# Moving the stationary operands of a two-layer decoder trunk to a pool of their own in SBUF

## The chip, the cores and the metric

The kernel runs on one core of one Trainium2 chip. The metric is the device time of one execution in microseconds (us); lower is better. Three runs of the kernel before gave 948.11 us as their median (947.25 to 948.29).

## The reference

Two layers over 256 tokens of width 1024, all in float32. Every matrix product of a layer is, cut to what matters:

```python
h = rms_norm(x, norm_mix_pre)
proj = h @ w_in                       # 1024 x 8208: conv, retention, GLA inputs and three merge gates
y_a, y_b, y_c = short_conv(...), retention(...), gated_linear_attention(...)   # 512 wide each
merged = sum(sigmoid(gate_i) * (y_i @ w_branch_i))
x = x + rms_norm(merged @ w_out, norm_mix_post)
h = rms_norm(x, norm_ffn_pre)
x = x + rms_norm((silu(h @ w_gate) * (h @ w_up)) @ w_down, norm_ffn_post)      # 2816 wide
```

## The kernel before

The 256 tokens are two row tiles of 128, t = 0 and t = 1. A product keeps the activations stationary and streams the weights: `mm` (line 272) calls one matmul with a stationary block of 128 x 128 and a moving block of 128 x 512 weights (256 or 272 at the edge of a matrix).

Precision comes from splitting. Activations and weights each become a high part (`hi`, float32r) and the rest (`lo`), and each block of 128 rows takes three matmuls: hi x whi, hi x wlo, lo x whi (`piece`, line 379). So each of these matmuls has its own stationary load, and successive matmuls use the blocks hi[i], hi[i], lo[i], hi[i+1], ...

The stationary tiles are:

- `hT0hi`, `hT0lo`, `hT1hi`, `hT1lo`: the transposed activations of row tile 0 and 1, eight blocks of 128 x 128 each (4096 bytes in a partition), one buffer each. They hold the normalised h, and later the merged m.
- `yThi`, `yTlo`: transposed branch outputs and the SwiGLU activations, four blocks each (2048 bytes), four buffers each. The GLA factors (`factors`, line 740) borrow the same buffers.

`pair` (line 413) makes both kinds; `sb` (line 241) makes the scratch tiles and the GLA factors under the tags `yThi` and `yTlo`:

```python
def sb(tag, bufs, cols=512, dt=F32):
    return p1.tile([P, cols], dt, tag=tag, name=nm(tag), bufs=bufs)
def pair(kt, tag, bufs):
    return [p1.tile([P, kt, P], F32R, tag=tag + s, name=nm(tag + s), bufs=bufs) for s in ("hi", "lo")]
```

Weights arrive in units of 512 KB (128 x 1024 float32) on SP's DMA queue into four `raw` buffers. ScalarE copies a unit to `whi` (line 189), VectorE writes the rest to `wlo` (line 191), in eight buffers each. A unit of 1024 columns feeds 12 matmuls, six for each row tile.

The order of TensorE's and SP's instructions is written out by the program itself (`Order`, a small planner that puts transposes and the chunk products of the branches between the pieces of the large products). ScalarE, VectorE and GpSimd are ordered by the framework. In most of the program a piece for t = 0 is followed by one for t = 1 on the same weights. In the closing of each half layer (`closing`) and the opening of the next (`skewed`) one row tile runs several pieces ahead of the other, so that stretches use hT0 alone or hT1 alone.

SBUF is laid out pool after pool, each pool's tags in the order of their first use: `const`, `rawp`, `wp`, `p1`, `sm`.

Of the kernel before, what the change touches and what calls it, by code (L numbers as in the profile page):

```python
# [10 lines left out]
F32R = mybir.dt.float32r  # L11
# [6 lines left out]
P = 128  # L18
# [202 lines left out]
def trunk(ctx: ExitStack, tc: tile.TileContext, ins, out):  # L221
# [2 lines left out]
    TS = range(NT)  # L224

    const = ctx.enter_context(tc.tile_pool(name="const", bufs=1))
    raw_pool = ctx.enter_context(tc.tile_pool(name="rawp", bufs=NRAW))
    wpool = ctx.enter_context(tc.tile_pool(name="wp", bufs=NSLOT))
    p1 = ctx.enter_context(tc.tile_pool(name="p1", bufs=1))
# [7 lines left out]
    def nm(s):  # L237
        cnt[0] += 1
        return f"{s}_{cnt[0]}"

    def sb(tag, bufs, cols=512, dt=F32):
        return p1.tile([P, cols], dt, tag=tag, name=nm(tag), bufs=bufs)

    def gt(cols=512):
        return sb("gt", 5, cols)

    def ut(cols=512):
        return sb("ut", 4, cols)

    def long():  # L250
        return sb("long", 6)
# [159 lines left out]
        return a, V.tensor_tensor(flat(lo[:, c0:c0 + n, :]), src, ho.bitcast(F32), ALU.subtract)  # L411

    def pair(kt, tag, bufs):
        return [p1.tile([P, kt, P], F32R, tag=tag + s, name=nm(tag + s), bufs=bufs) for s in ("hi", "lo")]

    def T_task(src, dst, wait, c0=0, n=4):
        yield wait
# [9 lines left out]
    def renorm(t, banks, w_post, w_next=None):  # L427
# [28 lines left out]
        if w_next is None:  # L456
            return
        yield CHAIN - HOLD
        hT[t] = pair(8, f"hT{t}", 1)
        for nb in range(2):  # L460
            yield O.acquire("tp")
# [83 lines left out]
    def first_norm(t, wait):  # L545
        yield wait
        hT[t] = pair(8, f"hT{t}", 1)
        hi, lo = hT[t]
        last = first_split[t]
        for c in range(2):  # L550
            yield O.acquire("ac")
            tp = transposed(x_sb[t][:, c * 512:(c + 1) * 512], 4, "ac")
            with tc.high_priority(offset=FIRST_PRI[t]):
                h = ut()
                V.tensor_tensor(h4(h), h4(tp), w_col[:, 4 * c:4 * c + 4].unsqueeze(2).to_broadcast([P, 4, P]), ALU.mult)
                last.append(split(h, hi, lo, 4 * c))
            O.release("ac", 1, 1.6)
            W.urgent = list(last[-1])
            W.split()
        W.hold = 1 - t  # L560
# [18 lines left out]
    for l in range(DEPTH):  # L579
# [337 lines left out]
        yT = [[None, None] for _ in range(3)]  # L917
# [19 lines left out]
        def conv_gate_task(t, b, conv):  # L937
            yield 1.5
            yield lambda: conv.done
            yield O.acquire("tp")  # L940
            tp = transposed(b)
            V.tensor_tensor(y_a[t], y_a[t], tp, ALU.mult)
            O.release("tp", 1, 2.0)
            yT[0][t] = pair(4, "yT", 4)
            split(y_a[t], *yT[0][t])
# [33 lines left out]
        for br in range(3):  # L979
            sig = {}  # L980
            for nb in range(2):
                for t, acc in enumerate(block()):
                    s = ut()
# [110 lines left out]
```

## Time and profile before

| what | value |
|---|---|
| median of the runs | 948.11 us (947.25 to 948.29) |
| the profiled execution | 948.13 us |
| its span, first to last instruction | 946.4 us |
| TensorE busy | 922.2 us, 97% of the span |
| VectorE, ScalarE, GpSimd busy | 61%, 49%, 11% |
| mean granted TensorE clock | 0.993 |
| moved by DMA | 165.67 MB, 175 GB/s on average |

The profile's times of matmuls overlap: one is shown with 0.39 us, but the next starts 0.23 us after it. How fast TensorE works is read from the distance of the starts in the timeline, or from a piece of the chain of waits, divided by its count.

### The profile page before, as it was taken

Reading aid. Unit: us, or ns where it says so; the run is one execution under the profiler, and the core shown is the slowest. Engines: PE = TensorE matmul, PEld = TensorE weight load, DVE = VectorE, ACT = ScalarE, POOL = GpSimd, SP = SyncE. Lnnn points to the kernel's source line nnn. Section 1 sums busy time; section 2 is a strip of 40 time slices with the busy share of each in tenths; the row PEclk is TensorE's granted clock in tenths of the full one; section 3 lists DMA queues with packets and bytes.
Section 4 is the critical chain, followed back from the end, with each engine's and each line's share of the span. In section 5 each row is a group of like instructions: output and inputs, shape, how many; then the busy total and the mean of one; then the engine's idle time right before and its main releaser. Section 6 shows DMA issues by size and latency. Waiting matters only on the chain.

```text
span 946.4 us, 12659 instructions
## 1 busy us (share of the span) xinstructions
PE 922.2 (97%) x4831; PEld 753.9 (80%) x4831; DVE 580.0 (61%) x830; ACT 462.1 (49%) x612; POOL 100.2 (11%) x142
## 2 busy tenths in 40 slices
PE   7889999999999999999989999999999999999997
PEld 5768888888888888888978778888888888888895
DVE  6789768555477655455466976775456765455443
ACT  5664364544456544444457536454444564444431
POOL 9022121002000000000010333010020000000000
PEclk9899999999999999999999999999999999999999
DMA  9985468868536767655679446788765476566621
GB/s 205 218 206 153 99 181 187 207 184 192 178 93 201 252 187 223 185 185 188 135 110 231 132 133 134 182 241 182 182 194 163 126 233 208 179 202 185 192 90 45
DMA packets 89485, 165.67 MB, mean 175 GB/s; under 512 B 5777, under 2 KB 15057, under 8 KB 89425
## 3 DMA queue, kind: packets, MB, share of 16 engines
q1 hardware_dynamic: 88192, 162.94, 64.6%
q0 software_dynamic: 656, 1.62, 0.7%
q8 instruction: 38, 0.62, 0.3%
q10 hardware_dynamic: 576, 0.30, 0.2%
q14 instruction: 23, 0.18, 0.1%
HBM read 163.79 MB, written 1.05 MB: 174 GB/s over the span
## 4 chain that ended last, share of the span: by engine, by line
PE 87%; DMA 5%; DVE 5%; issue 2%; ACT 1%; POOL 1%; POOLq 0%; DVEq 0%; ACTq 0%
PE mm L273 65%; PE ac L273 19%; DMA raw<-in_w_in_dram 5%; PE tp L279 3%; DVE wlo L191 2%; POOL gt L813 1%; ACT whi L189 1%; DVE yTlo L752 0%; DVE yThi L753 0%; DVE S L736 0%; DVE gt L811 0%; DVE x L447 0%; DVE gt L808 0%; DVE glo L690 0%; POOL rs L377 0%
## 5 line engine op out<-in xcount | busy, mean ns | idle before, releaser
L191 DVE TENSOR_TENSOR wlo<-raw,whi 128x1024 fp32r<-128x1024 f32 (+2 forms) x303 | 370.1, 1227 | 288.6 <-ACT whi L189 288.0
L189 ACT CAST whi<-raw 128x1024 fp32r<-128x1024 f32 (+2 forms) x303 | 314.7, 1040 | 348.1 <-PE mm L273 239.6
L273 PE MATMUL mm<-whi,hT1hi 128*128 128x512 f32 (+2 forms) x464 | 179.8, 388 | 1.8 <-ACT hT1hi L410 1.0
L273 PE MATMUL mm<-whi,hT0hi 128*128 128x512 f32 (+2 forms) x464 | 178.8, 385 | 1.1 <-ACT whi L189 1.1
L273 PE MATMUL mm<-wlo,hT0hi 128*128 128x512 f32 (+2 forms) x464 | 176.4, 381 | 0.5 <-DVE wlo L191 0.3
L273 PE MATMUL mm<-wlo,hT1hi 128*128 128x512 f32 (+2 forms) x464 | 176.8, 382 | 0.0
L273 PE MATMUL mm<-whi,hT1lo 128*128 128x512 f32 (+2 forms) x464 | 176.5, 380 | 0.2 <-DVE hT1lo L411 0.2
L273 PE MATMUL mm<-whi,hT0lo 128*128 128x512 f32 (+2 forms) x464 | 176.6, 381 | 0.0
L273 PEld LDWEIGHTS mm<-whi,hT1hi 128*128 128x128 f32 x464 | 87.8, 189 | 19.9 <-ACT hT1hi L410 1.2
L273 PEld LDWEIGHTS mm<-whi,hT0hi 128*128 128x128 f32 x464 | 88.6, 191 | 18.6 <-ACT whi L189 1.6
L273 PEld LDWEIGHTS mm<-wlo,hT0hi 128*128 128x128 f32 x464 | 88.6, 191 | 18.5 <-DVE wlo L191 1.9
L273 PEld LDWEIGHTS mm<-whi,hT1lo 128*128 128x128 f32 x464 | 87.5, 188 | 18.5 <-DVE hT1lo L411 0.5
L273 PEld LDWEIGHTS mm<-whi,hT0lo 128*128 128x128 f32 x464 | 88.4, 191 | 17.0
L273 PEld LDWEIGHTS mm<-wlo,hT1hi 128*128 128x128 f32 x464 | 87.5, 189 | 16.3
L273 PE MATMUL ac<-whi,yThi 128*128 128x512 f32 x176 | 71.3, 405 | 0.0
L273 PE MATMUL ac<-whi,yTlo 128*128 128x512 f32 x176 | 69.5, 395 | 0.0
L273 PE MATMUL ac<-wlo,yThi 128*128 128x512 f32 x176 | 69.3, 394 | 0.0
L377 POOL TENSOR_TENSOR rs<-rs,mhalf 128x1 f32<-128x1 f32 (+1 forms) x24 | 17.3, 719 | 442.5 <-DVE rs L439 441.2
L273 PEld LDWEIGHTS ac<-whi,yTlo 128*128 128x128 f32 x176 | 33.1, 188 | 7.7
L273 PEld LDWEIGHTS ac<-wlo,yThi 128*128 128x128 f32 x176 | 33.3, 189 | 6.8
L273 PEld LDWEIGHTS ac<-whi,yThi 128*128 128x128 f32 x176 | 33.2, 189 | 6.7
L273 PE MATMUL mm<-whi,yThi 128*128 128x512 f32 x96 | 38.2, 398 | 0.0
(169 smaller groups left out, 898.1 us busy)
## 6 DMA issues: line engine op xcount, KB each, us to landing
raw<-in_w_in_dram SPq DMA_DIRECT2D x123, 512.0 KB, 4.9
raw<-in_w_ffn_gate_dram SPq DMA_DIRECT2D x44, 512.0 KB, 3.7
raw<-in_w_ffn_up_dram SPq DMA_DIRECT2D x44, 512.0 KB, 4.3
raw<-in_w_ffn_down_dram SPq DMA_DIRECT2D x44, 512.0 KB, 3.8
raw<-in_w_out_dram SPq DMA_DIRECT2D x16, 512.0 KB, 4.0
raw<-in_w_branch_a_dram SPq DMA_DIRECT2D x8, 512.0 KB, 8.7
raw<-in_w_branch_b_dram SPq DMA_DIRECT2D x8, 512.0 KB, 4.1
raw<-in_w_branch_c_dram SPq DMA_DIRECT2D x8, 512.0 KB, 3.5
```

The source lines that it names most:

```text
L189: nc.scalar.copy(hi[:, c], raw[:, c])
L191: nc.vector.tensor_tensor(lo[:, c], raw[:, c], hi[:, c].bitcast(F32), ALU.subtract)
L273: T.matmul(acc, lhsT, rhs, start=start, stop=stop)
L279: T.transpose(acc, src, ident)
L377: return G.tensor_tensor(v, v, mhalf[:, :n], ALU.pow)
L813: last = G.tensor_tensor(a, a, b, ALU.add)
```

## The change

A pool `stat` is opened between `const` and `rawp`. All tiles of `pair`, and those of `sb` whose tag begins with `yT`, are taken from it. Tags, sizes and numbers of buffers stay.

```diff
     const = ctx.enter_context(tc.tile_pool(name="const", bufs=1))
+    stat = ctx.enter_context(tc.tile_pool(name="stat", bufs=1))
     raw_pool = ctx.enter_context(tc.tile_pool(name="rawp", bufs=NRAW))
...
     def sb(tag, bufs, cols=512, dt=F32):
-        return p1.tile([P, cols], dt, tag=tag, name=nm(tag), bufs=bufs)
+        return (stat if tag[:2] == "yT" else p1).tile([P, cols], dt, tag=tag, name=nm(tag), bufs=bufs)
...
     def pair(kt, tag, bufs):
-        return [p1.tile([P, kt, P], F32R, tag=tag + s, name=nm(tag + s), bufs=bufs) for s in ("hi", "lo")]
+        return [stat.tile([P, kt, P], F32R, tag=tag + s, name=nm(tag + s), bufs=bufs) for s in ("hi", "lo")]
```

No instruction moves: on all five engines the built programs have the same instructions in the same order with the same waits (PE, DVE, ACT, POOL and SP alike). Only addresses differ. The first byte of each tile in its partition, in the two built programs, and how far that lies past a multiple of 512 bytes (the size of one stationary block):

| tile | before | past 512 | after | past 512 |
|---|---|---|---|---|
| hT0hi, hT0lo | 132608, 136704 | 0 | 38400, 42496 | 0 |
| hT1hi, hT1lo | 141888, 145984 | 64 | 46592, 50688 | 0 |
| yThi (four, 2048 apart) | 197248 | 128 | 54784 | 0 |
| yTlo (four, 2048 apart) | 205440 | 128 | 62976 | 0 |
| raw (four, 4096 apart) | 38400 | 0 | 71168 | 0 |
| whi (eight, 4096 apart) | 54784 | 0 | 87552 | 0 |
| wlo (eight, 4096 apart) | 87552 | 0 | 120320 | 0 |
| ut (four, 2048 apart) | 120320 | 0 | 153088 | 0 |
| xs | 150080, 154208 | 64, 96 | 166464, 170592 | 64, 96 |
| qkT, gt, long, ghi, glo | from 158336 | 128 | from 174720 | 128 |
| S, nw, const, sm | | | not moved | |

So hT1, yThi and yTlo are the only tiles whose distance past a multiple of 512 changes; each 512-byte block of a tile has its tile's distance.

## Rows read from the trace of the kernel before

**Rows 1.** The page: span, busy time and share, granted clock in tenths
```profile
span 946.4 us, 12659 instructions
...
PE 922.2 (97%) x4831; PEld 753.9 (80%) x4831; DVE 580.0 (61%) x830; ACT 462.1 (49%) x612; POOL 100.2 (11%) x142
...
PEclk9899999999999999999999999999999999999999
```
**Rows 2.** What TensorE waited for: us in total, times, longest us
```profile
PE tp L279 <- ACT ut L595: 4.9, 1, 4.9
PE ac L273 <- ACT gaT L676: 2.6, 1, 2.6
...
PE mm L273 <- DVE hT1lo L411: 0.2, 1, 0.2
```
**Rows 3.** The chain that ended last, by time: start us, us, what
```profile
8.42 7.97 DMA raw<-in_w_in_dram
...
46.67 9.37 DMA raw<-in_w_in_dram
...
201.00 58.52 PE mm L273 x252
...
476.80 10.45 DMA raw<-in_w_in_dram
```
**Rows 4.** TensorE's groups by shape: count | busy us, mean ns | idle before
```profile
L273 PE MATMUL mm<-whi,hT1hi 128*128 128x512 f32 x400 | 161.6, 404 | 1.8 <-ACT hT1hi L410 1.0 <-ACT long L595 0.8
L273 PE MATMUL mm<-whi,hT0hi 128*128 128x512 f32 x400 | 159.1, 398 | 1.1 <-ACT whi L189 1.1
...
L273 PE MATMUL ac<-whi,yThi 128*128 128x512 f32 x176 | 71.3, 405 | 0.0
...
L273 PE MATMUL mm<-whi,yThi 128*128 128x512 f32 x96 | 38.2, 398 | 0.0
...
L273 PE MATMUL mm<-whi,hT0hi 128*128 128x256 f32 x48 | 15.1, 314 | 0.0
...
L273 PE MATMUL ac<-whi,hT1hi 128*128 128x512 f32 x32 | 13.0, 406 | 0.0
```
**Rows 5.** Timeline of TensorE, first layer's `w_out` product: start us, us, instruction
```profile
269.02 0.60 PE L279 MATMUL tp<-ident,xs 128*128 128x128 f32 x4
269.37 0.48 PE L273 MATMUL ac<-whi,hT0hi 128*128 128x512 f32 x1
269.69 0.40 PE L273 MATMUL ac<-wlo,hT0hi 128*128 128x512 f32 x1
...
272.23 0.39 PE L273 MATMUL ac<-whi,hT0hi 128*128 128x512 f32 x1
...
276.31 0.40 PE L273 MATMUL ac<-whi,hT1hi 128*128 128x512 f32 x1
276.54 0.39 PE L273 MATMUL ac<-wlo,hT1hi 128*128 128x512 f32 x1
...
280.97 0.39 PE L273 MATMUL ac<-whi,hT1lo 128*128 128x512 f32 x1
```
**Rows 6.** Timeline of TensorE, first branch product: start us, us, instruction
```profile
184.66 0.39 PE L273 MATMUL mm<-whi,yThi 128*128 128x512 f32 x1
...
195.82 0.39 PE L273 MATMUL mm<-whi,hT0hi 128*128 128x512 f32 x1
```
**Rows 7.** Timeline of TensorE, a w_in product, row tiles in turn
```profile
127.75 0.39 PE L273 MATMUL mm<-whi,hT1hi 128*128 128x512 f32 x1
...
129.15 0.39 PE L273 MATMUL mm<-whi,hT0hi 128*128 128x512 f32 x1
...
130.53 0.39 PE L273 MATMUL mm<-whi,hT1hi 128*128 128x512 f32 x1
```
**Rows 8.** Busy us of each engine from 201.0 to 259.5, clock, DMA share, GB/s
```profile
201.00:259.50 58.50, 58.50 (x255) 47.31 (x254) 29.34 (x29) 25.58 (x28) 6.91 (x4) 1.00 0.69 185
```
**Rows 9.** Timeline of all engines at 130 us: a matmul and stationary loads
```profile
130.30 0.39 PE L273 MATMUL mm<-whi,hT0lo 128*128 128x512 f32 x1
130.31 0.19 PEld L273 LDWEIGHTS mm<-whi,hT1hi 128*128 128x128 f32 x1
...
130.54 0.19 PEld L273 LDWEIGHTS mm<-wlo,hT1hi 128*128 128x128 f32 x1
```
**Rows 10.** Timeline of TensorE, last gate product, 256 columns wide
```profile
451.04 0.28 PE L273 MATMUL mm<-whi,hT1hi 128*128 128x256 f32 x1
...
452.46 0.28 PE L273 MATMUL mm<-whi,hT0hi 128*128 128x256 f32 x1
...
453.90 0.28 PE L273 MATMUL mm<-whi,hT1hi 128*128 128x256 f32 x1
```

## The prediction, made before the changed kernel ran

> **What bounds the kernel now.** I read the page first: TensorE is busy 922 of 946 us at nearly full granted clock [rows 1]. The table of TensorE's waits comes next: twelve entries of one wait each, from 4.9 us down to 0.2, 17.7 us together [rows 2]. The chain of waits then shows where the end is set: apart from weight DMAs in the first 56 us and at the change of layers, it consists of long pieces of matmuls, such as 252 of them in 58.52 us [rows 3]. So the time is the number of matmuls times the distance between their starts, and only something that alters that distance matters.
>
> That distance is what to look at. [...] The piece holds products on hT0, hT1 and yT, and no engine is short there: VectorE 29.3 us, ScalarE 25.6 us of 58.5, DMA 0.69 [rows 8].
>
> The timeline then tells the three stationary operands apart. In one product (same function, same kind of weights, same width) hT0 alone goes from 272.23 to 276.31, 18 matmuls in 4.08 us: 226.7 ns each. Directly behind it hT1 alone goes from 276.54 to 280.97, 19 distances in 4.43 us: 233.2 ns [rows 5]. yT alone takes 48 matmuls from 184.66 to 195.82: 232.5 ns [rows 6]. At 256 columns the two row tiles differ as well, but the other way round: 12 on hT1 take 1.42 us (118.3 ns), 12 on hT0 1.44 us (120.0 ns) [rows 10]. The next stationary load starts with the running matmul, 10 ns after it, and so reads SBUF while the weights stream out of it [rows 9]. What differs between the three operands is where they lie: hT0 at a multiple of 512 bytes, hT1 64 bytes past one, yT 128 past one. All weight tiles lie at multiples of 512.
>
> I read this as two reads of SBUF that get in each other's way by their relative position. [...] It isn't the accumulator: all eight blocks of a tile, weights in any of the 16 weight buffers, and other accumulators show the same 226 to 227 ns once hT0 has run alone for some ten matmuls.
>
> **The change part by part.** No instruction is added, removed or moved, and no wait differs. No DMA moves past another on any queue. Only three operands change their position against the weights: hT1 and yT come to lie as hT0 does, at a multiple of 512. hT0, the weights and the sources of the transposes (ut, xs, gt, long) keep theirs.
>
> *The term that pays.* Matmuls with 512 columns: hT0 and hT1 have three groups each of 400 and of 32, that is 2592; yT three groups each of 176 and of 96, 816; together 3408 [rows 4]. They come in 107 uninterrupted stretches (my count in the timeline); the first of each waits for its own load, as the 320 ns from 269.37 to 269.69 show [rows 5], and the last is cut off by what follows, so about 3200 distances count. If all are locked as hT0 alone is, each loses 232.2 - 226.7 = 5.5 ns: 3200 x 5.5 = 17.6 us.
>
> *What is taken off.* The 226.7 isn't there at once. Behind four transposes, the eleven distances from 269.69 to 272.23 take 2.54 us, 46 ns more than at 226.7 [rows 5]. Each of the 107 stretches starts so: 107 x 0.046 = 4.9 us. In the first 56 us and at the layer change, the weight DMA ends last [rows 3]; some 150 matmuls there only wait longer for it: 150 x 5.5 ns = 0.8 us. The 256-wide matmuls on hT1, 3 x 48 as on hT0 [rows 4], become as slow as hT0's: 144 x 1.7 ns = 0.2 us. Left: 17.6 - 4.9 - 0.8 - 0.2 = 11.7 us.
>
> *What hides nothing.* A faster TensorE asks for weights 2% sooner. In the long piece the DMA share goes from 0.69 to about 0.71, and VectorE and ScalarE stay at half [rows 8], so I price a new wait for weights at nothing. If that cover failed, all of the gain would be lost, not more. The 17.7 us of TensorE's waits stay.
>
> *Bounds.* No row shows a stationary tile low in SBUF next to weights that lie just above it, and part of `wlo` now lies beyond 131072 bytes. From below I bound the distance by the 226.7 ns of hT0 for every matmul, without any start of a stretch: 17.6 us gained. From above, by the worst lock that the rows show, 233.2 ns for all: 3200 x (233.2 - 232.2) = 3.2 us lost. I take the value next to hT0, since the position against the weights becomes exactly hT0's.
>
> The profiled execution took 948.13 us, 1.7 beyond its span and as long as the median of 948.11. So 946.4 - 11.7 + 1.7 = 936.4 us.
>
> [...]
>
> **The rivals.**
>
> [...]
>
> *No lock when tiles alternate.* In the w_in product where hT0 and hT1 take turns, six matmuls on hT1 take 1.40 us (233.3 each) and six on hT0 1.38 (230 to 231.3) [rows 7]: hT0 doesn't reach 226.7 there. I put that down to the phase that hT1 leaves behind. If instead any change of tile restarts it, every product would run at about 231.3: 3200 x 0.9 = 2.9 us gained, 945.2.
>
> [...]
>
> *Only h gains* (yT is locked by something of its own, since its buffers change every four blocks): 2592 / 3408 of the gain, 8.9 us: 939.2.
>
> **How the numbers follow.** My forecast has 0.68 (931 to 941 us), only h gains 0.07, no lock 0.07, no say 0.08, slower 0.10. This measurement tells some 0.2%, 1.9 us, from no change. Faster by more than that: 0.68 + 0.07 and most of "no lock", 0.81. Within it: 0.09. Slower: 0.10. The range leaves out the no-change and slower cases, 0.18 together: from 929, a little below 17.6 us gained, to 947.
>
> **What would show it.** Right: the stretch of 252 matmuls takes about 57.2 us; hT1 alone and yT alone show 226 to 227 ns a start after some ten matmuls; the mean times of the groups on hT1hi and yThi (404 and 405 ns [rows 4]) fall towards the 0.39 us of the locked hT0 rows [rows 5]; the waits stay near 17.7 us; the 256-wide matmuls show 120 ns on both tiles. Wrong: distances on hT1 or yT at 232 to 234 as before (position isn't it), or at 226.7 with new waits on `whi` or `wlo` that eat the gain (the cover failed), or hT0's own distances above 227 (the new neighbourhood).

## The result, and the profile after

The changed kernel took 939.74 us (median of three, 938.26 to 940.09) against 948.11: a ratio of 0.990, 95% interval 0.9876 to 0.9923. The forecast was 936.4 us. Two things are to be explained: that the distance between matmuls did what was forecast, almost to the nanosecond, and that 3.3 us of the gain are missing all the same. One execution among all that follow (the third of e10_rel32) took 1300.14 us at a mean granted clock of 0.654, and the comparisons leave it out.

The page of the profile after, the same lines as [rows 1]:

```profile
span 938.4 us, 12659 instructions
...
PE 913.2 (97%) x4831; PEld 756.3 (81%) x4831; DVE 578.9 (62%) x830; ACT 462.8 (49%) x612; POOL 99.4 (11%) x142
...
PEclk9879999999999999999999999999999999999999
```

TensorE is busy 9 us less for the same 4831 instructions, and one of the 40 slices, the third, has a lower clock than before (7 against 9). The timeline of TensorE in the product of [rows 5], each row a start in us, how long the matmul is shown, and the instruction:

```profile
273.84 0.39 PE L274 MATMUL ac<-wlo,hT0hi 128*128 128x512 f32 x1
...
277.69 0.39 PE L274 MATMUL ac<-whi,hT1hi 128*128 128x512 f32 x1
...
282.23 0.39 PE L274 MATMUL ac<-whi,hT1lo 128*128 128x512 f32 x1
```

hT0 alone: 17 distances in 3.85 us, 226.5 ns, as before. hT1 alone: 20 in 4.54 us, 227.0 ns, where [rows 5] had 233.2. The pace no longer changes where the one hands over to the other. The product on yT of [rows 6]:

```profile
187.73 0.39 PE L274 MATMUL mm<-whi,yThi 128*128 128x512 f32 x1
...
198.61 0.39 PE L274 MATMUL mm<-whi,hT0hi 128*128 128x512 f32 x1
```

48 matmuls in 10.88 us: 226.7 ns, before 232.5. The mixed stretch of [rows 3] in the chain of waits (start, us, what), in the first and in the second layer:

```profile
203.78 57.18 PE mm L274 x252
...
659.27 57.18 PE mm L274 x252
```

57.18 us against 58.52, 226.9 ns a matmul; 57.2 was forecast. And the 256-wide product of [rows 10], which was to get slower on hT1:

```profile
449.25 0.28 PE L274 MATMUL mm<-whi,hT1hi 128*128 128x256 f32 x1
...
450.69 0.28 PE L274 MATMUL mm<-whi,hT0hi 128*128 128x256 f32 x1
...
452.13 0.28 PE L274 MATMUL mm<-whi,hT1hi 128*128 128x256 f32 x1
```

12 on hT1 take 1.44 us, 120.0 ns (before 118.3), 12 on hT0 the same 1.44.

The other end of the account: the first stretch of 252 begins at 203.78, 2.78 us later than before [rows 3], although some 600 matmuls of 512 columns lie ahead of it. TensorE's two longest waits (us, times, longest) grew a little against [rows 2]; all its waits together went from 17.7 to 18.4 us:

```profile
PE tp L280 <- ACT ut L596: 5.8, 1, 5.8
PE ac L274 <- ACT gaT L677: 3.3, 1, 3.3
```

and behind the second of them, which ends at 59.15 us, the granted clock is down. A row for each window of 4 us: window, length, the busy time of TensorE, its weight loads, VectorE, ScalarE and GpSimd (with the count of instructions), the granted clock, the DMA share and GB/s:

```profile
52.00:56.00 4.00, 3.84 (x18) 2.75 (x16) 2.52 (x4) 3.96 (x6) 0.00 (x0) 1.00 1.02 162
56.00:60.00 4.00, 0.85 (x2) 0.50 (x2) 1.33 (x2) 2.12 (x4) 0.00 (x0) 0.80 0.99 264
60.00:64.00 4.00, 4.00 (x10) 2.56 (x10) 2.75 (x8) 2.89 (x7) 1.91 (x2) 0.50 0.71 227
64.00:68.00 4.00, 4.00 (x11) 2.90 (x10) 3.30 (x5) 1.66 (x6) 3.09 (x3) 0.50 0.74 211
68.00:72.00 4.00, 4.00 (x18) 3.23 (x17) 2.34 (x4) 2.37 (x4) 0.00 (x0) 0.92 0.19 63
```

TensorE works 0.85 of 4 us from 56 to 60. In windows of 1 us its granted clock is 1.00 from 57 to 58, 0.71 from 58 to 59, 0.50 from 59 to 60 and still from 67 to 68, and 1.00 again from 69; at 0.50, matmuls of 512 columns start 0.43 us apart.

TensorE's timeline tells how much of the time is lost where. The last matmul ahead of that wait, the first behind it, and the next transposes of `gt`, before and after the change:

```profile
54.41 0.39 PE L273 MATMUL mm<-whi,hT1lo 128*128 128x512 f32 x1
57.38 0.69 PE L273 MATMUL ac<-wa,gaT 17*128 17x256 f32 x2 [2.58 <-ACT gaT L676]
...
67.70 0.60 PE L279 MATMUL tp<-ident,gt 128*128 128x128 f32 x4
```
```profile
55.45 0.39 PE L274 MATMUL mm<-whi,hT1lo 128*128 128x512 f32 x1
59.15 1.22 PE L274 MATMUL ac<-wa,gaT 17*128 17x256 f32 x2 [3.31 <-ACT gaT L677]
...
72.20 0.60 PE L280 MATMUL tp<-ident,gt 128*128 128x128 f32 x4
```

The changed kernel is 1.04 us late ahead of the wait, 1.77 behind it and 4.50 at the transposes. From there to the end of the span it takes 866.2 us where the kernel before took 878.7: 12.5 us are gained.

### The profile page after: what moved, and what is told of

The parts are those of the page before. It is cut to its first block, busy times and chain, and to the rows that moved or that the text cites. A ratio compares the mean times of both kernels' runs of the same rounds, so it can differ in the third digit from the quotient of the medians.

```text
span 938.4 us, 12659 instructions
## 1 busy us (share of the span) xinstructions
PE 913.2 (97%) x4831; PEld 756.3 (81%) x4831; DVE 578.9 (62%) x830; ACT 462.8 (49%) x612; POOL 99.4 (11%) x142
## 4 chain that ended last, share of the span: by engine, by line
PE 87%; DMA 5%; DVE 4%; issue 2%; POOL 1%; ACT 1%; POOLq 0%; DVEq 0%; ACTq 0%
PE mm L274 65%; PE ac L274 19%; DMA raw<-in_w_in_dram 5%; PE tp L280 3%; DVE wlo L191 2%; POOL gt L814 1%; ACT whi L189 0%; DVE yTlo L753 0%; DVE yThi L754 0%; DVE S L737 0%; DVE x L448 0%; DVE gt L812 0%; DVE gt L809 0%; PE ac L280 0%; POOL rs L378 0%
## 5 line engine op out<-in xcount | busy, mean ns | idle before, releaser
L274 PE MATMUL mm<-wlo,hT1hi 128*128 128x512 f32 (+2 forms) x464 | 174.8, 377 | 0.0
```

What stands on the lines that cost most here:

```text
L274: T.matmul(acc, lhsT, rhs, start=start, stop=stop)
```

## The experiments

The theory is that the steady distance between starts is set by where the stationary tile lies against the weights, modulo some power of two in bytes. The first rivals are that the low place itself pays, and that an operand's own alignment does. All times stand beside runs of the kernel before on the same chip, 947.99 to 950.03 us in the median. The name in brackets is the run's; a row `x252` is the mixed stretch in the chain (start us, us, what), and a stand is a time in which TensorE waits.

**The same alignment without the low place (e1_mid).** The pool is opened behind the weights instead of in front of `raw`:

```diff
-    stat = ctx.enter_context(tc.tile_pool(name="stat", bufs=1))
     raw_pool = ctx.enter_context(tc.tile_pool(name="rawp", bufs=NRAW))
     wpool = ctx.enter_context(tc.tile_pool(name="wp", bufs=NSLOT))
+    stat = ctx.enter_context(tc.tile_pool(name="stat", bufs=1))
```

> The stationary pool opened behind the weights instead of behind the constants: raw, whi and wlo stay where they were before, hT0, hT1 and yT lie at 120320 to 153087, all at multiples of 512. Theory (position of the stationary operand against the weights, modulo 512 bytes): the 252-matmul stretch takes 57.2 us as after the change, hT1 alone and yT alone show 226.7 ns a start; 940 us if the clock falls at 57 us as after the change, 935 if it does not. Rival (lying low, away from the weights' old place, is what pays): as before, 58.5 us for the stretch and 948 us.

Measured: 936.09 us (935.31 to 937.08), ratio 0.9872 (0.9857 to 0.9887). In the chain:

```profile
200.43 57.18 PE mm L274 x252
```

The full gain with raw and weights where they were. The low place has no part in it.

**All stationary tiles 64 bytes off (e2_rel64).** As in e1_mid, with a gap in front of the pool:

```diff
+    gap = ctx.enter_context(tc.tile_pool(name="gap", bufs=1))
+    gap.tile([P, 16], F32, tag="gap", name="gap")
     stat = ctx.enter_context(tc.tile_pool(name="stat", bufs=1))
```

> As e1_mid, with 64 bytes left free in front of the stationary pool: hT0, hT1 and yT all lie 64 bytes past a multiple of 512, the weights at multiples of 512. Theory (position against the weights): every large product goes at hT1's old 233.3 ns, also hT0 alone and yT alone; the stretch takes 252 x 233.3 = 58.8 us; about 3190 x (233.3 - 227.8) = 17.5 us more than after the change, 952 to 957 us. Rival (only the three operands lying at different distances from each other costs, through restarts of the phase): 226.7 ns and 935 to 940 us.

Measured: 953.48 us, ratio 1.0052 (1.0037 to 1.0067): slower than the kernel before, as forecast.

```profile
203.54 58.80 PE mm L276 x252
```

58.80 us / 252 = 233.3 ns for a stretch that holds hT0, hT1 and yT, and on the timeline hT0 alone goes at 233.3 too: it has taken over hT1's old distance. The tile that was fast before the change is slow at the other position, so it isn't the row tile or the accumulator.

**Everything 64 bytes off (e3_abs64).** The same gap, but in front of the low pool of the changed kernel, so that the weights move along:

> As after the change, with 64 bytes left free in front of the stationary pool: stationary operands and weights all lie 64 bytes past a multiple of 512. Theory (position against the weights): as after the change, 226.7 ns, 57.2 us for the stretch, 935 to 940 us. Rival (an operand that does not begin at a multiple of 512 costs more by itself): 233 ns, 58.8 us for the stretch, 952 to 957 us.

Measured: 935.21 us, ratio 0.9865 (0.985 to 0.9879).

```profile
200.99 57.17 PE mm L276 x252
```

No operand begins at a multiple of 512 here, or of 128, and nothing is lost. It's the position of the two against each other.

**128 bytes off (e6_rel128).** The gap of e2_rel64 with 32 floats:

> As e1_mid with 128 bytes free in front of the stationary pool: all stationary tiles 128 bytes past a multiple of 512, weights at multiples. Theory (position against the weights): every large product goes as yT did before the change, 232.5 ns, and the time is 3190 x (232.5 - 227.8) = 15 us above e1_mid, about 951 us. Rival (only 64 bytes hurt, yT's 232.5 ns came from changing between tiles): 227 ns, 936 us.

Measured: 950.87 us, ratio 1.0022 (1.0003 to 1.0041).

```profile
202.66 58.80 PE mm L276 x252
```

58.80 us for the mixed stretch (233.3 ns). On the timelines all distances of 512-wide matmuls that follow one another average 232.7 ns here and 233.3 in e2_rel64: as forecast from yT.

**256 bytes off (e7_rel256).** The gap has 48 floats (192 bytes), and the conv table `cw` is moved into it; it takes 64 more:

> As e1_mid with the stationary tiles 256 bytes past a multiple of 512 (192 bytes free and the small conv table in front of them). No row so far tells this distance. If the pattern of SBUF repeats every 256 bytes: 226.7 ns, 936 us. If only multiples of 512 are good: 232 to 234 ns, 951 to 953 us. [...]

Measured: 936.41 us, ratio 0.9868 (0.9839 to 0.9896).

```profile
199.77 57.18 PE mm L276 x252
```

The same as at 0, 226.9 ns: it fits a pattern that repeats after 256 bytes, and lying farther apart did not bring the distance below the one at 0.

**64 bytes the other way (e8_relm64).** The pool low and at multiples of 512, the gap between it and `raw`:

```diff
     stat = ctx.enter_context(tc.tile_pool(name="stat", bufs=1))
+    gap = ctx.enter_context(tc.tile_pool(name="gap", bufs=1))
+    gap.tile([P, 16], F32, tag="gap", name="gap")
     raw_pool = ctx.enter_context(tc.tile_pool(name="rawp", bufs=NRAW))
```

> The stationary pool low as after the change, at multiples of 512, with 64 bytes free between it and the weights, so that the weights lie 64 bytes past a multiple of 512 and the stationary tiles 64 bytes before the weights' grid. If the loss depends only on how far apart the two are: as e2_rel64, 233.3 ns, 953 us. [...]

Measured: 939.45 us, ratio 0.9899 (0.9878 to 0.9921).

```profile
200.21 57.70 PE mm L276 x252
```

57.70 / 252 = 229.0 ns, not the 233.3 of 64 bytes forward: the sign counts.

The gaps also push the scratch tiles behind the pools along. It isn't they: in the built programs of e2_rel64, e3_abs64 and e8_relm64 `ut` begins at byte 153152 in all three, and the tiles behind it lie alike, yet the stretch takes 58.80, 57.17 and 57.70 us.

**192 bytes off, forward (e12_rel192)**, which is the same as 64 back if the pattern has 256 bytes:

> As e1_mid with 192 bytes free in front of the stationary pool: all stationary tiles 192 bytes past a multiple of 512. Theory (the steady distance depends on the position against the weights modulo 256 bytes, so 192 past is the same as 64 before): as e8_relm64, a repeating 229, 232, 226 ns with 229.0 on average, 3190 x (229.2 - 227.8) = 4.5 us above e1_mid, 939 to 941 us. Rival (what counts is which tile lies before which, or the place in SBUF, and 229 ns in e8_relm64 came from its low pool): 233 ns as for 32, 64 and 128 bytes in this place, 951 to 953 us.

Measured: 939.25 us, ratio 0.9924 (0.9883 to 0.9964).

```profile
201.75 57.70 PE mm L276 x252
```

The same 229.0 ns to the last digit, in another place of SBUF. With e7_rel256 this makes two pairs that lie 256 bytes apart and agree; 64 and 192, which lie 128 apart, don't.

**32 bytes back and forward (e9_relm32, e10_rel32).** The gaps of e8_relm64 and e2_rel64 with eight floats:

> The stationary pool low, at multiples of 512, with 32 bytes free between it and the weights: stationary tiles 32 bytes before the weights' grid (the same as 224 past it, if the pattern repeats every 256 bytes). Theory (the steady distance between starts depends on the position modulo 256 bytes: 226.7 ns at 0, 233.3 at 64, 232.5 at 128, 229 at 192): between the neighbours, 226.7 to 229 ns, 936 to 940 us. If the loss goes in steps of 64 bytes: either 226.7 or 229 exactly. If there is a better place than 0 at all, it is most likely here, since the loss falls from 128 over 192 to 0: below 226.7 ns and below 935 us.

> As e1_mid with 32 bytes free in front of the stationary pool: all stationary tiles 32 bytes past the weights' grid. Theory (position modulo 256 bytes): between 226.7 ns at 0 and 233.3 at 64, about 230 ns and 943 us. If the loss goes in steps of 64 bytes: 226.7 ns and 936 us, or 233.3 ns and 952 us.

Measured: 951.7 us, ratio 1.0028 (1.0013 to 1.0043), and 954.92 us, ratio 1.0066 (1.0035 to 1.0097). Two rows, 32 back and 32 forward:

```profile
202.25 58.80 PE mm L276 x252
```
```profile
203.34 58.80 PE mm L276 x252
```

The theory of both, that 32 bytes would lie between their neighbours, was wrong; 233.3 ns was named for 32 forward only in case the loss goes in steps. It is 233.3 ns on either side of 0: the good place is narrow, not the bottom of a slope, and no better place was found. Steps below 32 bytes, and 96 and 160, were not tried.

**The changed kernel once more (e5_again).**

> The changed kernel itself, on the chip of these runs. Theory (the clock falls at 57 us because TensorE stands 3.3 us there, and the length of that stand varies with when the weights land): where its stand is 2.7 us or less, as in e1_mid, the clock stays and the time is 935 to 937 us; where it is 3.3 us, the clock falls and the time is 939 to 940. Rival (the low place of the pools itself brings the fall about): the fall in every run, 939 to 940 us, against 936.1 for e1_mid.

Measured: 936.88 us (935.61 to 938.90), ratio 0.988 (0.9859 to 0.99). The profiled execution is the fastest of the four, 935.61 us; the same windows as above, 56 to 64:

```profile
56.00:60.00 4.00, 2.70 (x12) 1.44 (x10) 2.47 (x4) 3.30 (x9) 0.00 (x0) 1.00 1.01 279
60.00:64.00 4.00, 3.82 (x16) 2.71 (x16) 3.96 (x7) 3.70 (x9) 3.76 (x3) 1.00 0.73 232
```

The clock stays, and the stand that lasted 3.31 us before has 1.30:

```profile
56.02 0.39 PE L274 MATMUL mm<-whi,hT1lo 128*128 128x512 f32 x1
57.71 0.69 PE L274 MATMUL ac<-wa,gaT 17*128 17x256 f32 x2 [1.30 <-ACT gaT L677]
...
67.98 0.60 PE L280 MATMUL tp<-ident,gt 128*128 128x128 f32 x4
```

The stretches of 252 begin 4.23 and 4.49 us earlier than in the first profile of the changed kernel:

```profile
199.55 57.17 PE mm L274 x252
...
654.78 57.17 PE mm L274 x252
```

Between 72 and 470 us the two executions run in step, matmul for matmul. So the same program loses 4.2 us or doesn't, all of it between 56 and 72 us. Ahead of the stand the first profile is even 0.57 us ahead (55.45 against 56.02), behind it 1.44 late, at the transposes of `gt` 4.22: 2.0 us are the longer stand itself, 2.8 what follows with the clock down. The fall isn't in every execution of the changed kernel, as the rival would have it.

The length of the stand, on which the theory rested, doesn't decide. In e8_relm64 TensorE stands 2.70 us at the same place and the clock stays; in e12_rel192 it stands 2.24 us and the clock falls (each the matmul behind the stand, and the window from 60 us):

```profile
57.83 0.69 PE L276 MATMUL ac<-wa,gaT 17*128 17x256 f32 x2 [2.70 <-ACT gaT L679]
60.00:64.00 4.00, 3.94 (x17) 2.79 (x16) 3.97 (x7) 3.69 (x9) 3.63 (x3) 1.00 0.73 210
```
```profile
57.79 0.69 PE L276 MATMUL ac<-wa,gaT 17*128 17x256 f32 x2 [2.24 <-ACT gaT L679]
60.00:64.00 4.00, 4.00 (x10) 2.51 (x10) 3.44 (x6) 3.55 (x8) 2.74 (x3) 0.50 0.76 226
```

The clock also falls there in the traces of e2_rel64 (behind 2.28 us) and e6_rel128 (2.33), whose matmuls are no faster than before the change, and of e7_rel256 (2.65), e9_relm32 and e10_rel32. In the chains of the first four, three matmuls of the next large product take 1.29 us, 0.43 each, as at 0.50 in the first profile of the changed kernel; in e10_rel32 twelve, from 61.93 us, take 4.77; in e5_again six take 1.38. So neither a faster TensorE nor the low place, which of these e9_relm32 alone has, is needed for it. What decides is open.

**Keeping TensorE busy in that stand (e4_fill).** Twelve matmuls that nobody reads, into the bank that the next product overwrites:

```diff
-            z = bank("ac")[:, :256]
+            zb = bank("ac")
+            if (l, t) == (0, 0):
+                for _ in range(12):
+                    T.matmul(zb, hT[1][0][:, 0, :], flat(mlev[:, 0:4, :]), start=True, stop=True)
+            z = zb[:, :256]
             mm(z, gaT[t], wa, True, True)
```

> As after the change, with 12 matmuls of 512 columns (constants streamed over a block of hT1, into the bank that the next product overwrites; nobody reads their result) in the 3.3 us in which TensorE stands at 56 us. Theory (the gain that is missing, 4 to 5 us, is a fall of the granted clock that follows on this idle time): the clock stays at full speed from 42 to 498 us, and the time falls by 4 to 5 us against the change, to about 935 us. Rival (the clock falls for another reason, or the weights' DMA is what is late there): the clock falls all the same or the time stays at 940 us.

Measured: 936.32 us (935.18 to 936.46), ratio 0.987 (0.9854 to 0.9886). The clock stayed up there (1.00 in every window of 4 us from 56 to 72 us), but it also did in e1_mid and e5_again (1.00 in the same windows), which have no filling and the same time; and at the layer change, where it was expected to stay as well, it fell at 484 us as in e5_again: 18 matmuls of the chain, from 485.11 us, take 3.58 us, in e5_again 4.00 at a mean clock of 0.59 from 484 to 488. That the filling prevents the fall is not shown. With three stands filled (e11_fill3):

```diff
+    def filler(acc, lhs, n, early=False):
+        for _ in range(n):
+            T.matmul(acc, lhs[:, 0, :], idle.bitcast(F32R) if early else flat(mlev[:, 0:4, :]), start=True, stop=True)
...
+                filler(zb, hT[1][0], 8)
...
-            tp = transposed(xs[:, half[nb]])
+            tp = transposed(xs[:, half[nb]], fill=(hT[0][0], 8 if change[0] and (t, nb) == (1, 0) else 0))
...
-            tp = transposed(qk)
+            tp = transposed(qk, fill=(hT[0][0], 14 if (l, t) == (0, 0) else 0, True))
```

> The changed kernel with matmuls whose result nobody reads in three stands of TensorE: 14 at 22 us (3.5 to 6 us long), 8 at 56 us (1.3 to 3.3 us), 8 at the change of layers (2.2 us). Theory (the falls of the granted clock that follow on these stands cost time): no stretch at half clock behind the first 16 us or fewer of them, 1.7 us gained at the layer change (3.4 us at half clock), up to 3 at 28 to 36 us if the weights' DMA leaves it, and a smaller spread between runs: 932 to 935 us. Rival (the weights' DMA sets the pace there, so the clock costs nothing): 935 to 937 us, as the changed kernel in e5_again.

Measured: 936.43 us (935.06 to 936.99), ratio 0.9869 (0.9847 to 0.9891). The windows from 24 to 36 us, e11_fill3 first, then e5_again:

```profile
24.00:28.00 4.00, 1.76 (x11) 1.23 (x9) 1.70 (x2) 1.46 (x2) 2.08 (x5) 1.00 1.01 100
28.00:32.00 4.00, 4.00 (x30) 3.74 (x29) 1.27 (x2) 1.52 (x2) 0.00 (x0) 1.00 1.01 247
32.00:36.00 4.00, 0.58 (x5) 0.38 (x4) 3.76 (x12) 3.23 (x5) 0.00 (x0) 1.00 0.95 188
```
```profile
24.00:28.00 4.00, 0.00 (x0) 0.00 (x0) 0.70 (x2) 1.40 (x2) 1.67 (x4) 0.81 1.02 91
28.00:32.00 4.00, 3.88 (x16) 3.69 (x17) 1.18 (x2) 1.61 (x4) 0.00 (x0) 0.50 0.99 224
32.00:36.00 4.00, 3.70 (x23) 3.16 (x22) 3.79 (x11) 2.51 (x5) 0.00 (x0) 0.84 0.98 194
```

In these windows the filled kernel keeps its clock at 1.00, finishes the same matmuls sooner and then stands from 32 to 36 us, with 0.58 us of work: the DMA share is 0.95 to 1.02 in all six windows. Behind that stand its clock falls as well, to 0.57 on average from 36 to 40 us. At the start the weights' DMA sets the pace, and the low clock from 28 to 32 us cost e5_again nothing that the medians show: the time of e11_fill3 is the one that the rival gave, 935 to 937 us. The layer change may have gained: the stretches of 252 lie 455.23 us apart in e5_again (654.78 - 199.55) and 453.93 in e11_fill3:

```profile
200.30 57.17 PE mm L274 x252
...
654.23 57.17 PE mm L274 x252
```

That is 1.3 us of the 1.7 expected, in one execution of each; without filling and at the same position the distance is 455.49 in the first profile of the changed kernel and 454.29 in e7_rel256, so the gain isn't clear of their spread. The medians (936.43 and 936.88) don't tell the two kernels apart either. No version was found that beats the changed kernel by more than the spread of its runs.

## Why the prediction was right, point by point

*The bound.* TensorE's distance between starts was the time: with it down, 8.0 us of span went although TensorE's waits grew from 17.7 to 18.4 us.

*The distance.* hT0's 226.7 ns was taken as what all three would get. hT1 alone got 227.0, yT 226.7, the mixed stretch 226.9. The reason was right too, and the experiments sharpen it: the position against the weights counts (e2_rel64 against e3_abs64), modulo 256 bytes, not 512 as my table of addresses suggested (e7_rel256, e12_rel192 with e8_relm64). That the two reads of SBUF get in each other's way is one reading of this, which no run tests: `raw`, `whi` and `wlo` always moved together, and what inside SBUF or TensorE loses the time was not seen. All four tiles being at the same position isn't enough, as e2_rel64 shows at 233.3 ns.

*The size.* I had 3200 distances and 17.6 - 4.9 = 12.7 us; the 232.2 ns from which I took 226.7 are the 58.52 us of [rows 3] divided by 252, at a granted clock of 1.00 [rows 8]. In the two traces some 3190 matmuls of 512 columns directly follow another; their mean distance went from 232.0 to 227.8 ns: 3190 x 4.2 = 13.4 us. The starts of stretches, taken off with 46 ns each, are the 1.1 ns that the mean lies above 226.7: 3.5 us in all, not 4.9.

*The 256-wide matmuls* got slower as forecast, hT1 from 118.3 to 120.0 ns.

*The start of the program* is the term that was mis-sized. It was to keep 0.8 us from the gain; in the profiled execution of the first three it gained nothing up to 72 us and lost 4.5 us more; behind it 12.5 us were gained, where the forecast had 11.7. The step that failed is that nothing was priced behind the waits: their 17.7 us did stay, within 0.7, but I took the stands of the start from one trace, and asked neither how much the weights' landing varies nor what the clock does behind a stand. Of the 4.5 us, 1.0 was lost ahead of the stand, 0.7 is the longer stand (3.31 us for 2.58), and 2.7 follow behind it, where the clock is at 0.50 for some nine us. TensorE waits there for a copy (`gaT`) that ScalarE makes (from 58.84 us) only behind the cast of a weight unit (from 57.89), and that unit landed at 57.79 us, before the change at 56.04 [rows 3]:

```profile
47.73 10.06 DMA raw<-in_w_in_dram
```

Why it landed later in that execution isn't settled; e5_again has the same program without the fall, at 935.61 us. So the fall is told here as what followed on the stand, and not as shown to be caused by it. The other two of the first three runs, 938.26 and 939.74 us, have no trace, and that they lost their time in the same place isn't shown.

*What I named as a sign and isn't one:* the mean times of the groups. hT1hi, [rows 4], now reads:

```profile
L274 PE MATMUL mm<-whi,hT1hi 128*128 128x512 f32 x400 | 160.7, 402 | 2.8 <-ACT long L596 1.8 <-ACT hT1hi L411 1.0
```

402 ns instead of 404, while the distance on hT1 alone fell by 2.7%. The mean of overlapping times holds the first matmuls behind each break (0.48 us) and those at half clock (0.63); the distance of the starts is what must be read.

*The rivals.* "No say" (0.08), that addresses do nothing, fell with e2_rel64: the same 252 matmuls took from 57.17 to 58.80 us by position alone. "No lock when tiles alternate" fell with the mixed stretch at 226.9. "Only h gains" fell with yT at 226.7. "Slower" (0.10), that the new neighbourhood costs more, fell with e1_mid and the changed kernel at the same 57.18 us in two places of SBUF.

## What to carry to other kernels

Where every matmul loads its own stationary block, divide a long uninterrupted stretch of the chain by its count, and compare with the distance on each operand alone (here 232.2 ns against 226.7 on hT0); if two operands of one product show two distances, look at their addresses before looking at engines. Here one aligned pool took 0.9 to 1.2% off a kernel whose TensorE was 97% busy, and a gap of 32 bytes lost it again. For float32r matmuls of 512 columns with a load each, put stationary and moving tiles at the same offset modulo 256 bytes (226.9 ns here, against 229.0 to 233.3 at the other offsets), and check this whenever a small tile is added in front of them; other shapes have to be measured, as the 256 columns below show. And the clock can be down behind a stand in one execution and not in the next, as here 0.50 in the first profile and 1.00 in e5_again at the same place: look at the clock behind it, in more than one trace, before you explain a missing gain.

## What the runs showed of the hardware

With 512 float32r columns, a stationary load for every matmul and a granted clock of 1.00 (in the stretches of 252 before and after the change), the steady distance between starts was, by the stationary tile's position past the weights' in bytes modulo 256:

| position | 0 | 32 | 64 | 128 | 192 | 224 |
|---|---|---|---|---|---|---|
| ns, from the mixed stretch | 226.9 | 233.3 | 233.3 | 233.3 | 229.0 | 233.3 |

At 128 the average over the whole program is a little lower, 232.7. At position 0 the distance isn't in proportion to the columns: 226.7 ns on hT0 at 512, 120.0 at 256. By my estimate from these two, 106.7 ns go with 256 columns and some 13 ns a matmul with none. At 256 columns the order is another, and 0 is the slowest position of those read: 120.0 ns, against 118.3 at 64 before the change and 117.5 at 192 (e12_rel192, 12 on hT0 in 1.41 us):

```profile
450.05 0.28 PE L276 MATMUL mm<-whi,hT0hi 128*128 128x256 f32 x1
...
451.46 0.28 PE L276 MATMUL mm<-whi,hT1hi 128*128 128x256 f32 x1
```

What inside SBUF or TensorE makes the pattern is not settled by these runs.
